# Expert base pass of 64 slots in two column tiles, with overflow passes as short conditional blocks

## The chip, the cores and the metric

One core of one Trainium2 chip. The metric is the device time of one execution in microseconds. Of the runs of a kernel the median is given.

## The reference, cut to what matters

One encoder block on 256 tokens of width 1024: sparse attention and a Mamba-2 mixer, then a mixture of experts. The change touches only the last part: top 4 of 32 experts per token, each a clamped SwiGLU of 1024 to 2 x 1024 to 1024, in fp32.

```
logits = (xt @ w_router + b_router).astype(jnp.float32)
top_val, top_idx = lax.top_k(logits, TOPK_EXPERTS)
gates = jax.nn.softmax(top_val, axis=-1)
...
h = xt[tok] @ w1[e] + b1[e]
gate, up = h[:, :D_FF_EXPERT], h[:, D_FF_EXPERT:]
gate = jnp.minimum(gate, SWIGLU_LIMIT)
up = jnp.clip(up, -SWIGLU_LIMIT, SWIGLU_LIMIT)
act = (up + 1.0) * gate * jax.nn.sigmoid(SWIGLU_ALPHA * gate)
y = act @ w2[e] + b2[e]
return acc.at[tok].add(y * g[:, None])
```

The 1024 assignments are not spread evenly. With the reference's inputs experts 0 to 31 get 23, 11, 12, 101, 28, 32, 37, 2, 41, 13, 36, 3, 18, 9, 10, 138, 47, 66, 16, 27, 21, 34, 28, 23, 51, 20, 31, 43, 37, 11, 40 and 15 tokens.

## The kernel before, in words

Attention and mixer come first; they and the router end where the stage of the experts begins. The weights of the experts, 12 MB each and 384 MB in all, are read from HBM once. They come as slabs of 1 MB through a ring of 17 buffers (`wa`, `wb`, `wc`): eight slabs of w1 (128 rows of 2048 columns) and four of w2. SP starts every load in the order of the program; `load_more(8)` stands where the w1 slabs of an expert are done with (L1659) and `load_more(4)` where its w2 slabs are (L1674). A load waits until PE has read the slab that had its buffer.

For one expert, `onehot` marks on DVE which token sits in which slot, `gather` (L1385) multiplies the tokens with that on PE into `xg`, two experts at a time, half of it in each expert, and `slots` (L1397) gives the matrix `sT` and the gates `gs` for the way back. The base pass takes T = 32 slots. `first_mm` (L1426) multiplies each w1 slab with the 32 columns of tokens as the stationary operand; its four matmuls lie in the four column tiles of PE and write one PSUM bank, `X[0]`. `swiglu` runs on DVE and ACT, `turn` (L1432) transposes, `second_mm` (L1438) multiplies with w2, again in four column tiles, into `X[1]` and `Y[1]`. `scale_y` (L1450) applies the gates on ACT and DVE, and `scatter` (L1456) adds the result to the four accumulators on PE. The scatter of one expert is done in the next one, behind its first product.

Tokens beyond slot 32 go through overflow passes: pass 1 takes slots 32 to 63 (32 columns), pass 2 slots 64 to 127 and pass 3 slots 128 to 191 (64 columns each); a rare block `rest` (L1515), behind expert 2, takes what lies beyond 192. The passes run under `tc.If` on the expert's count, which every engine loads into a register. `if_more` (L1507) nests them: pass 2 stands inside pass 1 and pass 3 inside pass 2, once for the first halves (name "a": gather, first product, swiglu, turn) and once for the second (name "b": second product, scatter). `will` (L1504) gives PE a hint ahead of a branch, which side it will take.

The program is written out in the order in which each engine runs it (`manual_schedule`). Where a block is not taken, an engine jumps over it, waits for its own last result, and adds to its semaphore what the block would have added; who depends on a block waits for that engine to have passed it.

Of the kernel before, what the change touches and what calls it, by code (L numbers as in the profile page):

```python
# [22 lines left out]
KD = 8  # L23
# [35 lines left out]
T = 32  # L59
# [5 lines left out]
def shape_constants():  # L65
# [6 lines left out]
    iota = np.tile(np.concatenate([p % 32 + 1, p % 64 + 1, p + 1]).astype(f32)[None, :], (P, 1))  # L72
# [20 lines left out]
def kernel(ctx, tc, A, out, dbg=None):  # L93
# [44 lines left out]
    cst = const.tile([P, 672], F32, name="cst")  # L138
# [5 lines left out]
    iota128 = cst[:, 512:640]  # L144
    fold = cst[:, 640:672]
# [255 lines left out]
    def small_b():  # L401
        small(cst2, A["cst"][:, 672:1184])
        small(cst3, A["cst"][:, 1184:1568])
        small(cst[:, 128:672], A["cst"][:, 128:672])
# [961 lines left out]
    def wide(nm, dt=F32):  # L1366
        return buf(nm, [512], dt, 4, "t2k")

    def act_tiles(spare):
        return (wide("go"), wide("so")) if spare else (buf("gu", [512]), buf("sgm", [256]))  # L1370

    aT = buf("aT", [256])
    aTs = {1: buf("aT1", [256]), 2: buf("aT2", [512]), 3: buf("aT3", [512])}
    xo = buf("xo", [KD, M])
    b1v = b1s.rearrange("p (g c) -> p g c", g=2)
    LOW = {1: T, 2: M, 3: 2 * M}
# [43 lines left out]
    def first_bias(e, h, m):  # L1420
        for c in range(4):
            t, j = h[c * m // P], c * m % P
            mm(t[j:j + m, :], lhsT=selc[:, e:e + 1].to_broadcast([96, m]), rhs=b1v[:, :, c * 256:c * 256 + 256],
               start=True, stop=False, skip_group_check=True)

    def first_mm(w, x, h, m, k):  # L1426
        for c in range(4):
            t, j = h[c * m // P], c * m % P
# [3 lines left out]
    def turn(us, h, a):  # L1432
        for i, u in enumerate(us):
            for c in range(2):
                tr(h[i][:, cut(c)], u[:, cut(c)], ident)
            act(a[:, i * 256:i * 256 + 256], h[i][:, 0:256], AF.Copy)  # L1436
# [13 lines left out]
    def scale_y(y, gs, tag=None):  # L1450
        v = [wide(nm, F32R) if tag else buf(nm, [512], F32R, 2) for nm in ("yh", "yl")]
# [9 lines left out]
    counts, hints = {}, {}  # L1461

    def load_count(e):
        counts[e] = nc.values_load(cnt[0:1, e:e + 1], min_val=0, max_val=256)
        for p in (1, 2, 3):
            hints[e, p] = counts[e] > LOW[p]
# [8 lines left out]
    def own_gather(e, base):  # L1475
        g = buf("hgo", [2, M])
        onehot(g, e, iota64[:, 0:M], base)
        gather(g, xo, 0, X[1], M)

    def more_first(e, p):  # L1480
        if p == 1:
            put = put_hot(e, iota32, T, "o")
            x, h, m = xs(e)[:, :, T:M], (Y[0],), T
        else:
            put = put_hot(e, iota64, LOW[p], "o")
            own_gather(e, LOW[p])
            x, h, m = xo, (Y[0], X[1]), M
        first_bias(e, h, m)
        for k in range(KD):
            first_mm(wt[e * 12 + k], x, h, m, k)  # L1490
        us = [swiglu(t, True) for t in h]
        more[e, p] = slots(e, put, Y[1], str(p), 1)
        turn(us, h, aTs[p])

    def more_second(e, p, nhs):
        m = T if p == 1 else M
        ys = X[1], Y[1]
        for nh in nhs:
            for k in range(KD):
                second_mm(w2_part(e, k, nh), ys[nh], aTs[p], m, k)  # L1500
        for nh in nhs:
            scatter(nh, more[e, p][0], scale_y(ys[nh], more[e, p][1], "t2k"))

    def will(e, nm, p=1):  # L1504
        tc.mark_branch_hint_location("%s%d_%d" % (nm, e, p), hint=hints[e, p], engines=[mybir.EngineType.PE])

    def if_more(e, nm, f, *a, p=1):  # L1507
        with tc.If(counts[e] > LOW[p], label="%s%d_%d" % (nm, e, p)):  # L1508
            if p < 3:
                will(e, nm, p + 1)  # L1510
            f(e, p, *a)
            if p < 3:
                if_more(e, nm, f, *a, p=p + 1)

    def rest(e, dw):  # L1515
        own_gather(e, FULL)
        sg = slots(e, put_hot(e, iota64, FULL, "o"), Y[1], "2", 1)
        h, a = (X[0], Y[0]), aTs[2]
        first_bias(e, h, M)
        for k in range(KD):  # L1520
            nc.sync.dma_start(dw, w1[e, cut(k), :])
            first_mm(dw.rearrange("p (g c) -> p g c", g=2), xo, h, M, k)
        turn([swiglu(t, True) for t in h], h, a)
        y = X[1], Y[1]
        for q in range(4):
            v = dw.rearrange("p (a n) -> p a n", n=D)
            nc.sync.dma_start(v, w2[e, q * 256:(q + 1) * 256, :].rearrange("(a p) n -> p a n", p=P))
            for k in range(2 * q, 2 * q + 2):
                for nh in range(2):
                    second_mm(v[:, k % 2, nh * 512:(nh + 1) * 512], y[nh], a, M, k)  # L1530
        for nh in range(2):
            scatter(nh, sg[0], scale_y(y[nh], sg[1], "t2k"))

    def gate_values():
        for tt in range(2):
# [3 lines left out]
            ex = buf("rex", [NE], bufs=2)  # L1539
# [6 lines left out]
        gr = buf("gr", [2, NE])  # L1546
# [8 lines left out]
    def res(tt, hf, eng):  # L1555
        cs = slice(hf * 512, (hf + 1) * 512)
        tmp = wide("ftmp")
# [6 lines left out]
    fin = {}  # L1564

    def fin_split():
        r, o = wt["fin"], ring2()
        fin[0], fin[1] = o[:, 0:D], o[:, D:2 * D]
        o = ring2()
# [181 lines left out]
```

## Time and profile before

| | us |
|---|---|
| median of 3 runs | 1521.59 |
| lowest, highest | 1519.45, 1529.33 |
| the profiled execution | 1524.34 |
| its span, first to last instruction | 1522.5 |

The profile is of one execution. PE is the matmul side of TensorE, PEld its weight loads, DVE VectorE, ACT ScalarE, POOL GpSimd, SP the engine that starts the loads; a q behind a name is the sequencer of the engine, which waits and branches. A matmul in fp32 shows as two records. L12 is line 12 of the kernel.

### The profile page before, as it was taken

What the parts mean: (1) busy time and instruction counts of PE and PEld (TensorE: products, weight loads), DVE (VectorE), ACT (ScalarE), POOL (GpSimd) and SP (SyncE); (2) the same over time, 40 slices, a digit from 0 to 9 for tenths busy, and PEclk for the clock granted to TensorE, in tenths of its full rate; (3) what the DMA queues carried; (4) which work ended last, traced back from release to release, by engine and by line L of the source; (5) the groups of instructions that cost most, each with busy time, mean ns of one, the idle gap of its engine ahead of it and who ended that gap; (6) DMA issues with size and microseconds to landing.
All of it is one profiled execution on the core that took longest, in us unless ns stands there. A gap on an engine that the chain in (4) does not pass through costs nothing. (4 is left out here: it accounts for less than half of the span.)

```text
span 1522.5 us, 21278 instructions
## 1 busy us (share of the span) xinstructions
PE 1225.6 (80%) x8399; PEld 666.2 (44%) x8399; DVE 537.1 (35%) x1107; ACT 294.1 (19%) x508; POOL 172.1 (11%) x123
## 2 busy tenths in 40 slices
PE   6988989998768878787777788988867777778784
PEld 3778778886323333334323243433332323323331
DVE  5678689786311212122212112221121212212134
ACT  2465546543100101010100001011000001001011
POOL 2333135423000000000000000000000000000002
PEclk9889989999978999899998869989998989989896
DMA  9777446987995699999999905465899999999971
GB/s 305 227 216 255 159 161 203 307 290 304 372 409 220 245 414 415 412 412 415 413 413 414 407 31 221 193 252 215 323 415 415 412 414 415 414 413 370 386 316 43
DMA packets 127430, 480.89 MB, mean 316 GB/s; under 512 B 12635, under 2 KB 49643, under 8 KB 92406
## 3 DMA queue, kind: packets, MB, share of 16 engines
q1 hardware_dynamic: 122598, 472.40, 79.3%
q10 hardware_dynamic: 4624, 5.67, 1.2%
q8 instruction: 137, 2.24, 0.6%
q14 instruction: 71, 0.58, 0.1%
HBM read 475.00 MB, written 3.03 MB: 314 GB/s over the span
## 5 line engine op out<-in xcount | busy, mean ns | idle before, releaser
L1429 PE MATMUL px<-wb,xg 128*32 128x512 f32 x1080 | 143.1, 646 | 28.4 <-DMA wb<-in_w 24.4
L1459 PE MATMUL acc<-yh,sT 128*128 128x512 f32 x192 | 95.4, 497 | 50.2 <-PEq L1508 39.5
L1395 POOL TENSOR_TENSOR xg<-xg,modT 128x512 f32<-128x512 f32 x32 | 33.3, 1040 | 875.9 <-DVE xg L1393 875.9
L1412 DVE TENSOR_SCALAR gu<-px 128x256 f32<-128x256 f32 x32 | 13.6, 425 | 303.5 <-PE px L1429 303.5
L426 PE MATMUL pj<-uTh,wl 128*128 128x256 f32 x360 | 106.9, 297 | 5.4 <-DVE wl L305 2.9
L426 PE MATMUL pj<-uTh,wh 128*128 128x256 f32 x360 | 108.6, 302 | 0.4 <-ACT iqz L645 0.4
L305 POOL TENSOR_TENSOR wl<-wa,wh 128x1024 fp32r<-128x1024 f32 x34 | 87.8, 2583 | 178.6 <-ACT wh L304 150.4
L426 PE MATMUL pj<-uTl,wh 128*128 128x256 f32 x360 | 106.4, 295 | 0.0
L1453 DVE SCALAR_TENSOR_TENSOR yl<-px,gs,yh 128x512 fp32r<-128x512 f32 x48 | 36.0, 751 | 198.1 <-ACT yh L1452 194.2
L304 ACT ACTIVATE wh<-wa 128x1024 fp32r<-128x1024 f32 x75 | 78.7, 1057 | 107.3 <-PE pj L426 77.7
L1459 PE MATMUL acc<-yl,sT 128*128 128x512 f32 x192 | 92.7, 483 | 4.5 <-DVEq L1508 3.1
L1414 ACT ACTIVATE sgm<-gu 128x256 f32<-128x256 f32 x32 | 13.3, 416 | 397.0 <-DVE gu L1412 397.0
L1459 PEld LDWEIGHTS acc<-yh,sT 128*128 128x128 f32 x192 | 43.6, 227 | 97.1 <-issue 54.1
L1429 PEld LDWEIGHTS px<-wb,xg 128*32 128x32 f32 x1080 | 34.6, 115 | 116.3 <-issue 68.4
L1443 PE MATMUL px<-wb,aT 128*32 128x512 f32 (+1 forms) x376 | 70.3, 600 | 17.0 <-ACT aT L1436 8.9
L1429 PE MATMUL px<-wa,xg 128*32 128x512 f32 x504 | 73.3, 685 | 11.4 <-DMA wa<-in_w 8.8
L1393 DVE TENSOR_TENSOR xg<-py,sc 128x512 f32<-128x512 f32 x32 | 22.1, 692 | 170.1 <-PE py L1389 99.0
L426 PEld LDWEIGHTS pj<-uTh,wl 128*128 128x128 f32 x360 | 72.6, 202 | 8.2 <-POOL wl L305 3.5
L1389 PEld LDWEIGHTS py<-hg,n 128*128 128x128 f32 x512 | 71.1, 213 | 11.2 <-issue 6.2
L426 PEld LDWEIGHTS pj<-uTh,wh 128*128 128x128 f32 x360 | 72.7, 202 | 4.0 <-issue 2.9
L1389 PE MATMUL py<-hg,n 128*128 128x128 f32 x512 | 69.8, 294 | 5.5 <-issue 2.5
L1429 PE MATMUL px<-wc,xg 128*32 128x512 f32 x464 | 62.8, 656 | 13.4 <-DMA wc<-in_w 13.4
(442 smaller groups left out, 2069.2 us busy)
## 6 DMA issues: line engine op xcount, KB each, us to landing
wb<-in_w SPq DMA_DIRECT2D x201, 1024.0 KB, 19.1
wc<-in_w SPq DMA_DIRECT2D x92, 1024.0 KB, 20.1
wa<-in_w SPq DMA_DIRECT2D x91, 1024.0 KB, 18.4
wa<-in_w_in SPq DMA_DIRECT2D x24, 1024.0 KB, 6.9
wa<-in_w_mod SPq DMA_DIRECT2D x16, 1024.0 KB, 5.0
wa<-in_w_mod SPq DMA_DIRECT2D x16, 512.0 KB, 6.1
wa<-in_w_proj_b SPq DMA_DIRECT2D x4, 1024.0 KB, 5.2
wa<-in_w_proj_a SPq DMA_DIRECT2D x4, 1024.0 KB
```

Of the source, the lines that this page charges most:

```text
L304: i = act(xh, x, AF.Copy)
L305: eng.tensor_tensor(xl, x, xh.bitcast(F32), op=OP.subtract)
L426: mm(o, lhsT=a[:, k, :], rhs=b[:, k, :], start=(k == 0 and i == 0), stop=(k == KD - 1 and i == 2), skip_group_check=True)
L1389: mm(t[:, i * m:(i + 1) * m], lhsT=n2[:, tt, cut(k0 + i)], rhs=oh[:, tt, :], start=(tt == 0), stop=(tt == 1), skip_group_check=True)
L1393: V.tensor_tensor(o, t.rearrange("p (a s) -> p a s", a=n), sc2[:, ks].unsqueeze(2).to_broadcast([P, n, m]), op=OP.mult)
L1395: G.tensor_tensor(o, o, sh2[:, ks].unsqueeze(2).to_broadcast([P, n, m]), op=OP.add)
L1412: V.tensor_scalar(gt, h[:, 0:w], SWIGLU_LIMIT, None, op0=OP.min)
L1414: act(sg, gt, AF.Sigmoid, scale=SWIGLU_ALPHA)
L1429: mm(t[j:j + m, :], lhsT=x[:, k, 0:m], rhs=w[:, :, c * 256:c * 256 + 256], start=False, stop=(k == KD - 1), skip_group_check=True)
L1443: mm(y[m * j:m * j + m, :], lhsT=a[:, b:b + m], rhs=w, start=(k < n), stop=(k >= KD - n), skip_group_check=True)
L1453: V.scalar_tensor_tensor(v[1], y, gs, v[0].bitcast(F32), op0=OP.mult, op1=OP.subtract)
L1459: mm(acc[tt][nh], lhsT=sT[:, tt, :], rhs=y, start=False, stop=False, skip_group_check=True)
```

## The change

The base pass takes M = 64 slots: four matmuls of 64 columns for each w1 slab, in two column tiles, into two PSUM banks `X[0]` and `Y[0]`, two swiglus, two turns. Pass 1 is gone. Passes 2 and 3 are no longer nested and carry no hints: each is three blocks in the first half (`more_in`: gather and slots; `more_first` for either bank) and one block in the second (`more_second`), with an `If` of its own around each. Pass 2's first half stands directly behind the base's first product, then come the scatter of the expert before, the gather for the next pair and the slots, then pass 3's first half, then `load_more(8)`, then the turns and the second product. In the last expert the scaling of the base's result comes ahead of the overflow blocks. Some buffers change: the pair gather goes through `X[1]` in place of `Y[0]`, `hg`, `sT` and `gs` are single, and a temporary of the last step lies in the ring. A constant of 128 columns that nobody read is gone.

```diff
-    LOW = {1: T, 2: M, 3: 2 * M}
+    LOW = {2: M, 3: 2 * M}
...
-    def first_mm(w, x, h, m, k):
-        for c in range(4):
-            t, j = h[c * m // P], c * m % P
-            mm(t[j:j + m, :], lhsT=x[:, k, 0:m], rhs=w[:, :, c * 256:c * 256 + 256], start=False,
+    def first_mm(w, x, h, k, phs=(0, 1)):
+        for c in range(2 * phs[0], 2 * phs[-1] + 2):
+            j = c % 2 * M
+            mm(h[c // 2][j:j + M, :], lhsT=x[:, k, 0:M], rhs=w[:, :, c * 256:c * 256 + 256], start=False,
                stop=(k == KD - 1), skip_group_check=True)
...
-    def second_mm(w, y, a, m, k):
-        n = P // m
-        j = k % n
-        c, q = k % 2, k // 2
-        b = q // n * 256 + c * P + q % n * m
-        mm(y[m * j:m * j + m, :], lhsT=a[:, b:b + m], rhs=w, start=(k < n), stop=(k >= KD - n), skip_group_check=True)
+    def second_mm(w, y, a, k):
+        j = k % 2
+        b = k // 4 * 256 + k % 2 * P + k % 4 // 2 * M
+        mm(y[M * j:M * j + M, :], lhsT=a[:, b:b + M], rhs=w, start=(k < 2), stop=(k >= KD - 2), skip_group_check=True)
...
-    def more_first(e, p):
-        if p == 1:
-            put = put_hot(e, iota32, T, "o")
-            x, h, m = xs(e)[:, :, T:M], (Y[0],), T
-        else:
-            put = put_hot(e, iota64, LOW[p], "o")
-            own_gather(e, LOW[p])
-            x, h, m = xo, (Y[0], X[1]), M
-        first_bias(e, h, m)
+        more[e, p] = slots(e, put, Y[1], str(p), 1)
+
+    def more_first(e, p, ph):
+        h = X[1], Y[1]
+        first_bias(e, h, (ph,))
         for k in range(KD):
-            first_mm(wt[e * 12 + k], x, h, m, k)
-        us = [swiglu(t, True) for t in h]
-        more[e, p] = slots(e, put, Y[1], str(p), 1)
-        turn(us, h, aTs[p])
+            first_mm(wt[e * 12 + k], xo, h, k, (ph,))
+        turn(swiglu(h[ph], True), h[ph], aTs[p], ph)
...
-    def if_more(e, nm, f, *a, p=1):
-        with tc.If(counts[e] > LOW[p], label="%s%d_%d" % (nm, e, p)):
-            if p < 3:
-                will(e, nm, p + 1)
+    def if_more(e, p, f, *a):
+        with tc.If(counts[e] > LOW[p]):
             f(e, p, *a)
-            if p < 3:
-                if_more(e, nm, f, *a, p=p + 1)
+
+    def more_a(e, p):
+        if_more(e, p, more_in)
+        for ph in range(2):
+            if_more(e, p, more_first, ph)
...
-        us = [swiglu(h)]
-        if_more(e, "a", more_first)
-        load_more(KD)
+        us = [swiglu(t) for t in h]
+        more_a(e, 2)
         if not last:
-            will(e, "b")
             for v in late:
                 scatter(*v)
             if q < NE // 2:
                 pair_gather(q, e % 2)
-        sT, gs = slots(e, put, Y[1], "", 2)
-        turn(us, (h,), aT)
+        sT, gs = slots(e, put, Y[1], "", 1)
+        more_a(e, 3)
+        load_more(KD)
+        for ph in range(2):
+            turn(us[ph], h[ph], aT, ph)
         if not last:
             for k in range(KD):
                 for nh in range(2):
-                    second_mm(w2_part(e, k, nh), y[nh], aT, T, k)
+                    second_mm(w2_part(e, k, nh), y[nh], aT, k)
             late = [(nh, sT, scale_y(y[nh], gs)) for nh in range(2)]
-            if_more(e, "b", more_second, (0, 1))
+            for p in (2, 3):
+                if_more(e, p, more_second, (0, 1))
             load_more(3 if e == LATE else 4)
```

What PE's program has at the end of the base's first product, before; `wc` and `wb` are w1 slabs, `xg` the gathered tokens, L1508 the branch of an `If`, L1738 the hint:

```order
L1423 MATMUL px_3648<-b1s,selc 32x512
L1429 MATMUL px_3648<-wc,xg 32x512 x12
L1429 MATMUL px_3648<-wb,xg 32x512 x20
L1508 COMPARE_AND_BRANCH
L1505 REGISTER_ALU
L1738 BRANCH_PREFETCH_HINT
L1423 LDWEIGHTS selc
L1423 MATMUL py_3650<-b1s,selc 32x512
```

and now, with the first of the eight branches (L1489) and the first rows of its block:

```order
L1425 MATMUL px_3648<-wb,xg 64x512 x2
L1425 MATMUL py_3650<-wb,xg 64x512 x2
L1489 COMPARE_AND_BRANCH
L1385 MATMUL px_3649<-hgo,n_78 128x64 x16
L1397 LDWEIGHTS hpo
L1397 MATMUL py_3651<-identb,hpo 128x128
```

The slabs feed 64 columns into two banks, by turns, and the block behind the branch begins with the gather of pass 2.

Where the first half of the overflow ends and the scatter begins on PE, before; `go` is the activation of a pass, `acc` an accumulator:

```order
L1435 MATMUL py_3650<-cst,go 128x128 x2
L1435 MATMUL px_3649<-cst,go 128x128 x2
L1508 UNCONDITIONAL_BRANCH x4
L1505 REGISTER_ALU
L1738 BRANCH_PREFETCH_HINT
L1459 MATMUL acc_3644<-yh,sT 128x512
```

and now, where the third of three blocks in a row ends:

```order
L1489 COMPARE_AND_BRANCH
L1419 LDWEIGHTS selc
L1419 MATMUL py_3651<-b1s,selc 64x512
L1419 LDWEIGHTS selc
L1419 MATMUL py_3651<-b1s,selc 64x512
L1425 MATMUL py_3651<-wc,xo 64x512 x4
L1425 MATMUL py_3651<-wb,xo 64x512 x12
L1430 MATMUL py_3651<-cst,go 128x128 x2
L1489 UNCONDITIONAL_BRANCH x2
L1452 MATMUL acc_3644<-yh,sT 128x512
```

One join at the end of a nest has become three joins one behind the other, and the same stands once more behind the slots.

SP's program for one expert, before; L1018 and L127 start the loads of w1 and w2 slabs:

```order
L1508 COMPARE_AND_BRANCH x3
L1508 UNCONDITIONAL_BRANCH x4
L1018 DMA wb<-in_w 128x2048 x4
L127 DMA wb<-in_w 128x2x1024 x2
L127 DMA wa<-in_w 128x2x1024 x2
L1508 COMPARE_AND_BRANCH x3
```

and now:

```order
L1489 COMPARE_AND_BRANCH
L1489 UNCONDITIONAL_BRANCH x2
L1016 DMA wa<-in_w 128x2048 x4
L126 DMA wc<-in_w 128x2x1024 x4
L1489 COMPARE_AND_BRANCH
L1489 UNCONDITIONAL_BRANCH x2
L1489 COMPARE_AND_BRANCH
L1489 UNCONDITIONAL_BRANCH x2
L1016 DMA wb<-in_w 128x2048 x4
```

The eight loads stand behind the last of six branches, which waits for what PE does behind scatter, gather and slots; before, they stood behind one nest that PE passed ahead of these.

## Rows read from the trace of the kernel before

**Rows 1.** The page, busy tenths of the DMA engines in 40 equal slices.
```profile
DMA  9777446987995699999999905465899999999971
```

**Rows 2.** Windows: stretch, length, busy PE, PEld, DVE, ACT, POOL; clock, DMA share, GB/s.
```profile
820.00:850.00 30.00, 21.94 (x130) 7.05 (x130) 4.59 (x11) 2.07 (x4) 1.04 (x1) 0.85 1.02 414
...
970.00:1000.00 30.00, 24.55 (x188) 11.13 (x180) 8.57 (x21) 4.25 (x8) 1.04 (x1) 0.94 0.65 261
1000.00:1030.00 30.00, 26.78 (x192) 12.46 (x194) 5.42 (x17) 1.22 (x3) 1.04 (x1) 0.83 0.43 177
1030.00:1060.00 30.00, 25.13 (x150) 11.52 (x150) 6.28 (x16) 3.83 (x8) 1.04 (x1) 0.94 0.50 193
```

**Rows 3.** Waits of SP's queue from 440 us on: total, times, longest.
```profile
SPq L1018 <- PEq L1508: 324.2, 34, 42.2
```

**Rows 4.** PE's timeline, experts 14 and 15: start, length, instruction [idle before <-releaser].
```profile
811.03 0.40 PE L1423 MATMUL px<-b1s,selc 96*32 96x512 bf16 x4 [0.83 <-PEq L1508]
...
841.05 0.40 PE L1423 MATMUL px<-b1s,selc 96*32 96x512 bf16 x4 [0.83 <-PEq L1508]
...
845.78 1.06 PE L1429 MATMUL px<-wb,xg 128*32 128x512 f32 x8 [1.42 <-DMA wb<-in_w]
```

**Rows 5.** PE's timeline, a 64-column overflow pass and a 32-column base pass.
```profile
914.40 1.02 PE L1429 MATMUL py<-wb,xo 128*64 128x512 f32 x4
915.26 1.02 PE L1429 MATMUL px<-wb,xo 128*64 128x512 f32 x4
...
965.78 3.61 PE L1429 MATMUL px<-wc,xg 128*32 128x512 f32 x32
```

**Rows 6.** PE's timeline, expert 14: end of the scatter, gather, start of the second product.
```profile
831.32 0.39 PE L1459 MATMUL acc<-yl,sT 128*128 128x512 f32 x1
831.55 1.95 PE L1389 MATMUL py<-hg,n 128*128 128x128 f32 x16
...
834.43 0.97 PE L1443 MATMUL px<-wa,aT 128*32 128x512 f32 x2 [0.52 <-ACT aT L1436]
```

**Rows 7.** Timeline: the first matmul behind a skip, in experts 3, 7 and 14.
```profile
498.65 0.49 PE L1459 MATMUL acc<-yh,sT 128*128 128x512 f32 x1 [0.63 <-PEq L1508]
...
626.15 0.79 PE L1459 MATMUL acc<-yh,sT 128*128 128x512 f32 x1 [2.95 <-PEq L1508]
...
829.61 0.49 PE L1459 MATMUL acc<-yh,sT 128*128 128x512 f32 x1 [0.41 <-PEq L1508]
```

**Rows 8.** Line 1508, branches of PE's sequencer: shortest/median/longest ns.
```profile
L1508 PEldq COMPARE_BRANCH  x119: 68/309/6337, 380.0 to 1501.5; - x119
```

**Rows 9.** The page's groups: busy us, mean ns | idle before.
```profile
L1412 DVE TENSOR_SCALAR gu<-px 128x256 f32<-128x256 f32 x32 | 13.6, 425 | 303.5 <-PE px L1429 303.5
```

**Rows 10.** PE's timeline, a scatter in expert 16.
```profile
981.76 0.63 PE L1459 MATMUL acc<-yl,sT 128*128 128x512 f32 x1
982.19 0.63 PE L1459 MATMUL acc<-yh,sT 128*128 128x512 f32 x1
```

**Rows 11.** PE's timeline, expert 15: pass 1, gathers of passes 2 and 3, their second halves.
```profile
860.68 0.65 PE L1423 MATMUL py<-b1s,selc 96*32 96x512 bf16 x4
...
872.76 5.14 PE L1389 MATMUL px<-hgo,n 128*128 128x64 f32 x32 [0.52 <-DVE hgo L1381]
...
900.32 7.09 PE L1389 MATMUL px<-hgo,n 128*128 128x64 f32 x32 [0.47 <-ACT aT L1436]
...
944.55 1.94 PE L1443 MATMUL px<-wb,aT 128*64 128x512 f32 x8
...
954.16 1.94 PE L1443 MATMUL px<-wb,aT 128*64 128x512 f32 x8
```

**Rows 12.** The first matmuls of the experts (first and last start), behind expert 2, and b2.
```profile
L1423 PE MATMUL px<-b1s,selc x136: 379/389/637, 375.4 to 1479.5; 96*32 96x512 bf16 x128, 96*64 96x512 bf16 x8
...
447.09 0.62 PE L1423 MATMUL px<-b1s,selc 96*32 96x512 bf16 x4 [9.32 <-DVEq L1680]
...
L1694 PE MATMUL acc<-wa,gTs 32*128 32x512 f32 x8 | 6.9, 1038 | 0.3 <-DVE gTs L1691 0.3
```

More of the change, by code (lines that the diff above doesn't have):

```diff
@@ L1448, in w2_part, with scale_y @@
         return wt[e * 12 + KD + nh * 2 + k // 4][:, k % 4, :]
-    def scale_y(y, gs, tag=None):
-        v = [wide(nm, F32R) if tag else buf(nm, [512], F32R, 2) for nm in ("yh", "yl")]
+    def scale_y(y, gs, v=None):
+        v = v or [buf(nm, [512], F32R, 2) for nm in ("yh", "yl")]
         act(v[0], y, AF.Copy, scale=gs)
@@ L1459, in scatter @@
                 mm(acc[tt][nh], lhsT=sT[:, tt, :], rhs=y, start=False, stop=False, skip_group_check=True)
-    counts, hints = {}, {}
+    counts = {}
     def load_count(e):
         counts[e] = nc.values_load(cnt[0:1, e:e + 1], min_val=0, max_val=256)
-        for p in (1, 2, 3):
-            hints[e, p] = counts[e] > LOW[p]
     more = {}
@@ L1499, in more_second @@
             for k in range(KD):
-                second_mm(w2_part(e, k, nh), ys[nh], aTs[p], m, k)
+                second_mm(w2_part(e, k, nh), ys[nh], aTs[p], k)
         for nh in nhs:
-            scatter(nh, more[e, p][0], scale_y(ys[nh], more[e, p][1], "t2k"))
-    def will(e, nm, p=1):
-        tc.mark_branch_hint_location("%s%d_%d" % (nm, e, p), hint=hints[e, p], engines=[mybir.EngineType.PE])
-    def if_more(e, nm, f, *a, p=1):
-        with tc.If(counts[e] > LOW[p], label="%s%d_%d" % (nm, e, p)):
-            if p < 3:
-                will(e, nm, p + 1)
+            scatter(nh, more[e, p][0], scale_y(ys[nh], more[e, p][1], yo))
+    def if_more(e, p, f, *a):
+        with tc.If(counts[e] > LOW[p]):
             f(e, p, *a)
-            if p < 3:
-                if_more(e, nm, f, *a, p=p + 1)
+    def more_a(e, p):
+        if_more(e, p, more_in)
+        for ph in range(2):
+            if_more(e, p, more_first, ph)
     def rest(e, dw):
-        own_gather(e, FULL)
+        g = buf("hgo", [2, M])
+        onehot(g, e, iota64[:, 0:M], FULL)
+        gather(g, xo, 0, X[1], M)
         sg = slots(e, put_hot(e, iota64, FULL, "o"), Y[1], "2", 1)
         h, a = (X[0], Y[0]), aTs[2]
-        first_bias(e, h, M)
+        first_bias(e, h)
         for k in range(KD):
             nc.sync.dma_start(dw, w1[e, cut(k), :])
-            first_mm(dw.rearrange("p (g c) -> p g c", g=2), xo, h, M, k)
-        turn([swiglu(t, True) for t in h], h, a)
+            first_mm(dw.rearrange("p (g c) -> p g c", g=2), xo, h, k)
+        for i in range(2):
+            turn(swiglu(h[i], True), h[i], a, i)
         y = X[1], Y[1]
@@ L1626, in pair_gather @@
     def pair_gather(q, half):
-        gather(hg[q].rearrange("p t e s -> p t (e s)"), xg[q], 4 * half, Y[0], 2 * M)
+        gather(hg[q].rearrange("p t e s -> p t (e s)"), xg[q], 4 * half, X[1], 2 * M)
     def xs(e):
@@ L1701 @@
         for k in range(KD):
-            second_mm(w2_part(e, k, nh), y[nh], aT, T, k)
-        will(e, "b%d_" % nh)
-        if_more(e, "b%d_" % nh, more_second, (nh,))
-        scatter(nh, sT, scale_y(y[nh], gs))
+            second_mm(w2_part(e, k, nh), y[nh], aT, k)
+        v = scale_y(y[nh], gs)
+        for p in (2, 3):
+            if_more(e, p, more_second, (nh,))
+        scatter(nh, sT, v)
         if nh == 0:
```

74 lines of the change are left out of this document (35 added, 39 removed).

## The prediction

> **What bounds the kernel now.** I read the page's slices first, then the windows, then PE's timeline expert by expert. In the slices [rows 1] the sixteen DMA engines stand at nine tenths or more over most of the expert stage, which begins near 375 us, with holes near 480, 880 to 1080 and at the end. The windows say the same in numbers [rows 2]: 820 to 850 moves 414 GB/s with TensorE busy 21.94 of 30 us, while 970 to 1060 moves 177 to 261 GB/s with TensorE busy 24.6 to 26.8. So two regimes take turns: weights arrive at full rate and PE waits for them, or PE works and SP, which starts the loads, waits for PE to pass an `If` (324.2 us in 34 waits [rows 3]).
>
> In the first regime one expert takes what its loads take. Two starts, those of experts 14 and 15, lie 30.0 us apart (811.03 and 841.05), and inside the expert PE waits for each megabyte, 1.42 us before the slab at 845.78 [rows 4]. Twelve slabs of 1.05 MB at 414 GB/s make 30.4 us; I take that as the pace of the loads. A base pass is hidden while PE needs less than this for an expert, and sets the time where it needs more. That is the whole question.
>
> Which experts overflow follows from the reference's inputs: 20 of the 32 have at most 32 tokens, 9 have 33 to 64, and experts 3, 15 and 17 have 101, 138 and 66.
>
> [...] An fp32 matmul stands in the trace as two records.
>
> Products. The base's first product has 32 matmuls, 64 records, in either kernel. Four 64-column records follow the last four after 0.86 us (914.40, 915.26), so 64 take 13.7 us with two column tiles at work; 32 records of 32 columns took about 3.4 us (the row's 3.61 less the overlap with the next), so 64 took 6.9 [rows 5]. The second product has 32 records, so 6.9 us against 3.4. The base grows by 10.3 us for each of 32 experts, 330 us; the 12 passes over slots 32 to 63 go, each with the same 10.3 us and some waits. On PE's account that is a loss, since 20 experts never had that pass.
>
> The rest of an expert, from an undisturbed one [rows 6]: scatter 8 x 0.23 = 1.9; gather, slots, transposes and the wait for aT together 2.9 (831.55 to 834.43, less rounding), with 0.2 for two transposes more; bias 0.4, twice the 0.2 of four 32-column ones.
>
> Skips. An expert of up to 32 tokens passed two skips on PE, now eight, in groups of three, three and two. On the path not taken each engine first waits for its own last result, so PE is empty in a group. One skip that went well left PE idle 0.41 us (829.61), one followed by a second branch instruction 0.63 (498.65) [rows 7]; ahead of the next expert it was 0.83 [rows 4]. PE's branches take 309 ns in the median [rows 8]; with 0.2 for the semaphore step between two of them I count 0.5 for each further skip, so 1.4, 1.4 and 1.3: 4.1 us. Bounds: 1.6 if only the first of each group shows (0.41 + 0.41 + 0.83), and 2.5 more for every group that meets a slow branch, from 626.15, where the same skip left 2.95 instead of 0.41. I take 4.1, nearer to the quick rows, since the median is quick.
> [...]
>
> Sum for one expert: 0.4 + 13.7 + 1.4 + 1.9 + 2.9 + 0.2 + 1.4 + 6.9 + 1.3 = 30.1 us, already the pace of the loads, and two things are missing. First, the gather writes a buffer that the conditional blocks also read, so it waits until DVE has passed the first group; DVE stands there behind two swiglus now, not one. A swiglu is four DVE steps of some 0.42 us [rows 9], 1.7 us; two end about when PE has done its skips and the scatter. I take 0.5 us (bounds 0 and 1.7). Second, the clock. After short idle times the granted clock falls: at 981.76 and 982.19 the scatter steps by 0.43 us and not 0.23 [rows 10], and in 970 to 1060, where PE sets the pace, the mean granted clock is 0.94, 0.83 and 0.94 [rows 2]. I count one scatter per expert at 1.2 GHz, 1.5 us; bounds 0, and 5 if scatter, gather and transposes all run at half. So an interval of 32.1, taken as 32, and the loads lie beside it.
>
> The release of the eight w1 slabs moves behind scatter, gather, slots and six branches, some 6 us later in SP's program, with SP's next eight loads queued behind it. With PE as the bound this costs nothing: five slabs of the next expert are in the ring by then, and the three missing ones have the second product's 6.9 us and the first five slabs' 8.6 us to land. If PE is not the bound, the first expert alone holds its slabs some 10 us longer while the ring is full.
>
> Overflow from slot 64 on: four passes run, as now. One costs 27.6 us in its first half (two gathers at 872.76 and 900.32) and 9.6 in its second (944.55 to 954.16) [rows 11]; the split by column half exposes one more swiglu step chain, about 1 us net, and the skip time of some 2 us goes: 36 us each, 144.
>
> The path through PE: first expert at 375.4 [rows 12]; 31 intervals of 32 are 992, to 1367; overflow 144, to 1511; the jump over `rest` behind expert 2, which left PE idle 9.32 us, adds 8 beyond an ordinary group, to 1519; the eight b2 matmuls 6.9, to 1526. The last expert took 43.0 us (1479.5 to the span's end, 1522.5); it gains 10.3 of base work, loses some 3 of branch waits: 50, to 1576. Expert 0 has no scatter and the last two no gather, 5.6 us together: 1570. The profiled execution took 1524.34 us for its span of 1522.5, so 1572, and lies 2.75 above the median of the runs, 1521.59, so 1569.
>
> **Rivals.**
> A, the loads still set the pace. If the later skips of a group hide and the clock stays up, PE needs 28 us, under the loads' 30.4. Then the first expert (10 us) and the last (about 8) show, less some 8 of slow branches that go where PE sets the pace now: about 1530. For it: the sum without skips is 26 us. Against it: every row with a second branch has its gap, and the base, 20.6 us of products where 10.3 stood, leaves no room for a slow clock. [...]
>
> B, slow branches without the hints. Now 119 branches have a median of 309 ns but a maximum of 6337 [rows 8]. If one group in each expert meets that, PE loses 2.5 us more per expert: 32 x 2.5 = 80, so 1649. For it: slow ones exist even with hints. Against it: the jumps are short now, over one block of product, and not over three.
> [...] No run shows a short jump alone yet.
>
> C, faster. In the stretches that PE sets (experts 3, 15 to 17 and 21: five of the 12 removed passes) each pass that goes frees 10.3 us of products and some 7 of exposed steps (12.1 us from 860.68 to 872.76 less 6.9 of matmuls [rows 11], and a scatter of 1.9): 85 us. If the larger bases of the same experts and of the two or three behind them find their slabs landed and no skip gap, they give back some 60 of it: 25 us net, 1497. It decides only where PE's time for an expert stays under about 28 us. Against it: the experts that catch up behind expert 17 then need 10 us more each.
>
> **How the numbers follow.** Forecast 0.62, A 0.14, B 0.18, C 0.04, anything else 0.02. A measurement here tells about 1% from no change, 1506 to 1537. C is faster, 0.04; A and what lies under an interval of 31 us are the same, 0.15; the rest, 0.81, is slower. The forecast's own range is 1538 to 1615, intervals of 31 to 33.5. The range goes down through A to 1518 and up to B's 1650.
>
> **What would show it.** Right: ordinary experts start about 32 us apart from the first on; PE has hardly any wait for a slab in the base's first product; the DMA share is near 0.95, with a short hole in each expert; about 1.4 us idle on PE at each group of three; 64 records in 13.7 us. A is right if PE still waits for slabs all through. B is right if PE's branch row has many of several us. The forecast is wrong if starts lie 30.4 us apart, or if a group of branches leaves less than 0.7 us.

## The result, and the profile after

The changed kernel takes 1583.76 us in the median of four runs (1580.01 to 1584.52), the kernel before 1521.55 beside it: a ratio of 1.039, interval 1.035 to 1.043. It is slower by 62 us; 1569 was forecast, with a range that holds it. The profiled execution took 1584.52 for a span of 1582.7.

The page after, PE's busy time and the tenths of PE, granted clock and DMA in 40 slices:

```profile
PE 1337.2 (84%) x7095; PEld 769.5 (49%) x7095; DVE 541.4 (34%) x1115; ACT 291.0 (18%) x524; POOL 173.1 (11%) x123
...
PE   6788989998878898888888888888888888888884
...
PEclk9989989999997999999999989989999999999898
DMA  9667547974895479999999933472799999999970
```

PE is busy at eight tenths from the first expert to the last; the DMA row has its holes around the same experts as before [rows 1]. The windows of before [rows 2], and one of an ordinary stretch, in the same columns:

```profile
820.00:850.00 30.00, 26.31 (x128) 13.22 (x130) 4.60 (x12) 2.36 (x5) 1.04 (x1) 0.94 1.01 411
970.00:1000.00 30.00, 24.27 (x111) 8.81 (x111) 5.43 (x12) 4.79 (x10) 0.00 (x0) 1.00 0.72 280
1000.00:1030.00 30.00, 27.87 (x127) 10.96 (x127) 6.00 (x17) 2.21 (x4) 0.00 (x0) 1.00 0.34 140
1030.00:1060.00 30.00, 24.50 (x124) 11.92 (x124) 6.83 (x19) 2.76 (x6) 1.04 (x1) 0.98 0.90 363
1208.00:1238.00 30.00, 26.30 (x132) 12.98 (x131) 5.99 (x15) 2.62 (x7) 1.04 (x1) 1.00 1.02 415
```

At 820 PE has 26.31 us of work in 30 and not 21.94, and the clock stands at 0.94 to 1.00 where it had been 0.83 to 0.94. What is left of the 30 us is this, in PE's timeline of expert 21 (start, length, instruction, idle before and its releaser):

```profile
1208.11 0.43 PE L1419 MATMUL px<-b1s,selc 96*64 96x512 bf16 x2 [0.94 <-PEq L1489]
...
1208.54 1.08 PE L1425 MATMUL px<-wb,xg 128*64 128x512 f32 x4
1209.40 1.08 PE L1425 MATMUL py<-wb,xg 128*64 128x512 f32 x4
...
1223.61 0.47 PE L1452 MATMUL acc<-yh,sT 128*128 128x512 f32 x1 [1.11 <-PEq L1489]
1223.92 0.40 PE L1452 MATMUL acc<-yl,sT 128*128 128x512 f32 x1
1224.15 0.39 PE L1452 MATMUL acc<-yh,sT 128*128 128x512 f32 x1
...
1225.59 2.02 PE L1385 MATMUL px<-hg,n 128*128 128x128 f32 x16
...
1229.29 0.41 PE L1430 MATMUL px<-cst,gu 128*128 128x128 f32 x2 [1.53 <-PEq L1489]
...
1230.17 1.08 PE L1436 MATMUL px<-wa,aT 128*64 128x512 f32 x4 [0.26 <-ACT aT L1431]
...
1238.49 0.43 PE L1419 MATMUL px<-b1s,selc 96*64 96x512 bf16 x2 [1.18 <-PEq L1489]
```

Nothing waits for a slab. Three gaps are left, 1.11, 1.53 and 1.18 us, one at each group of skips; the scatter steps by 0.23 us, at a granted clock of 1.00 (1223.60 to 1225.60). PE's waits from 380 us on (total, times, longest), the branches (shortest/median/longest ns) and SP's wait that answers to [rows 3]:

```profile
PE px L1430 <- PEq L1489: 50.4, 31, 4.5
PE acc L1452 <- PEq L1489: 29.5, 27, 1.3
PE px L1419 <- PEq L1489: 27.7, 28, 1.2
```
```profile
L1489 PEldq COMPARE_BRANCH  x274: 70/208/3737, 388.7 to 1566.0; - x137
```
```profile
SPq L1016 <- PEq L1489: 536.1, 52, 47.2
```

The 60.2 us between the two profiled spans, by the first matmul of each expert (an interval runs from one expert's start to the next):

| | before | after | |
|---|---|---|---|
| start of expert 0 | 375.4 | 378.7 | +3.3 |
| 26 intervals without a long expert | 762.4 | 813.4 | +51.0 |
| expert 2, with the jump over `rest` | 33.1 | 37.6 | +4.4 |
| expert 3 (101 tokens) | 80.6 | 75.1 | -5.5 |
| expert 15 (138) | 122.8 | 109.5 | -13.3 |
| expert 17 (66) | 73.6 | 74.5 | +0.9 |
| expert 29, with the b2 matmuls | 31.5 | 39.7 | +8.2 |
| last expert, to the end | 43.0 | 54.2 | +11.2 |

The long experts gain 18 us; the 26 ordinary ones lose 51. Their mean goes from 29.32 to 31.28 us. Before, this mean was made of quick experts of 17 to 27 us and of slower ones, up to 49 us with pass 1; now the fastest of the 26 takes 29.65 us.

### The profile page after: what moved, and what is told of

It is laid out like the page before. It is cut to its first block, busy times and chain, and to the rows that moved or that the text cites. A ratio compares the mean times of both kernels' runs of the same rounds, so it can differ in the third digit from the quotient of the medians.

```text
span 1582.7 us, 19858 instructions
## 1 busy us (share of the span) xinstructions
PE 1337.2 (84%) x7095; PEld 769.5 (49%) x7095; DVE 541.4 (34%) x1115; ACT 291.0 (18%) x524; POOL 173.1 (11%) x123
## 5 line engine op out<-in xcount | busy, mean ns | idle before, releaser
L1425 PE MATMUL px<-wb,xg 128*64 128x512 f32 x540 | 148.3, 599 | 0.0
L1425 PE MATMUL py<-wb,xg 128*64 128x512 f32 x540 | 147.9, 598 | 0.0
L1408 DVE TENSOR_SCALAR gu<-px 128x256 f32<-128x256 f32 x32 | 13.6, 425 | 363.9 <-PE px L1425 363.9
L1436 PE MATMUL px<-wb,aT 128*64 128x512 f32 x288 | 84.1, 641 | 9.3 <-issue 3.9
L1425 PEld LDWEIGHTS py<-wb,xg 128*64 128x64 f32 x540 | 53.4, 138 | 64.2 <-issue 62.6
L1436 PE MATMUL py<-wb,aT 128*64 128x512 f32 x296 | 83.5, 620 | 0.0
L1425 PEld LDWEIGHTS px<-wb,xg 128*64 128x64 f32 x540 | 53.3, 139 | 57.3 <-issue 54.6
L1452 PE MATMUL acc<-yh,sT 128*128 128x512 f32 x128 | 54.9, 429 | 31.1 <-PEq L1489 29.5
L424 PEld LDWEIGHTS pj<-uTl,wh 128*128 128x128 f32 x360 | 71.7, 199 | 1.2 <-issue 0.8
L1385 PE MATMUL px<-hg,n 128*128 128x128 f32 x512 | 67.2, 286 | 5.1 <-DVEq L1489 3.9
L1385 PEld LDWEIGHTS px<-hg,n 128*128 128x128 f32 x512 | 62.9, 199 | 15.8 <-ACTq L1489 10.8
L1425 PE MATMUL px<-wa,xg 128*64 128x512 f32 x252 | 69.0, 604 | 0.0
```

The source lines that it names most:

```text
L424: mm(o, lhsT=a[:, k, :], rhs=b[:, k, :], start=(k == 0 and i == 0), stop=(k == KD - 1 and i == 2), skip_group_check=True)
L1385: mm(t[:, i * m:(i + 1) * m], lhsT=n2[:, tt, cut(k0 + i)], rhs=oh[:, tt, :], start=(tt == 0), stop=(tt == 1), skip_group_check=True)
L1408: V.tensor_scalar(gt, h[:, 0:w], SWIGLU_LIMIT, None, op0=OP.min)
L1425: mm(h[c // 2][j:j + M, :], lhsT=x[:, k, 0:M], rhs=w[:, :, c * 256:c * 256 + 256], start=False, stop=(k == KD - 1), skip_group_check=True)
L1436: mm(y[M * j:M * j + M, :], lhsT=a[:, b:b + M], rhs=w, start=(k < 2), stop=(k >= KD - 2), skip_group_check=True)
L1452: mm(acc[tt][nh], lhsT=sT[:, tt, :], rhs=y, start=False, stop=False, skip_group_check=True)
```

## The experiments

The kernel before was run again beside each experiment; its medians lie between 1520.7 and 1526.8 us, so a difference of a few microseconds between two experiments is not clear by itself.

**Fewer skips.** One `If` around each pass's first half.

```diff
-        if_more(e, p, more_in)
-        for ph in range(2):
-            if_more(e, p, more_first, ph)
+        if_more(e, p, more_all)
```

> The changed kernel with the three blocks of each overflow pass's first half under one If, so that an ordinary expert passes four skips in groups of one, one and two, where the changed kernel has eight in groups of three, three and two. Theory S (PE sets the pace, and each further skip costs PE about 0.5 us): PE's time for an ordinary expert falls by some 2 us, from 31.3 to 29.3, under the loads' 30.4, and the starts lie 30.4 to 30.6 us apart; 26 such intervals and the last expert give about 22 us, so 1555 to 1568. Rival R (the late release of the w1 slabs behind scatter, gather and slots sets the pace, and skips are only waited through): no change beyond 5 us, since the release stands where it stood. Rival B (slow branches without hints): the ten branches of over 1 us become about half as many, 10 us faster, and the ordinary interval without one stays above 30.

1538.88 us, 45 less, twice what was expected. Intervals have a median of 28.8 us, below the pace of the loads. The gap ahead of the scatter is gone altogether:

```profile
1180.23 0.47 PE L1452 MATMUL acc<-yh,sT 128*128 128x512 f32 x1
...
1182.88 2.02 PE L1385 MATMUL px<-hg,n 128*128 128x128 f32 x16 [0.56 <-DVEq L1489]
```

PE's sequencer had taken the single branch 9.9 us into the expert, at 1175.59, while matmuls were still queued until 1180.08; the join followed at 1180.12. In the changed kernel's expert 21 the first of three branches comes as early, at 1218.00, but the other two start only behind the matmuls' end, at 1222.69 and 1223.10. Part of what the missing gap gave is lost again in the row shown: the gather now waits 0.56 us for DVE to have passed its branch (27 such waits, 17.8 us together). Slow branches also became fewer, 6 of 14.5 us together against 9 of 19.0. That the interval falls under the pace of the loads (30.2 us, measured in the next pair) contradicts my floor; the next pair shows why.

**No overflow at all, wide and narrow base.** The blocks and their `If`s are taken out of the changed kernel, and out of the kernel before.

```diff
-        if_more(e, p, more_in)
-        for ph in range(2):
-            if_more(e, p, more_first, ph)
+        return
...
-            for p in (2, 3):
-                if_more(e, p, more_second, (0, 1))
```

> The changed kernel without any overflow block or its If: tokens beyond the first 64 of an expert are left out. Theory S: PE's time for an expert is then 27 to 28 us, less than the loads' 30.4, so after the first experts every interval is 30.4 us and PE waits for slabs again; 379 + 31 x 30.4 + 50 = 1371, with up to 8 for the jump behind expert 2: 1371 to 1385. Rival R: the release of the w1 slabs behind scatter, gather and slots still leaves holes in the transfers, and intervals stay above 31 us: 1395 or more. Rival W (the wide base alone is too long for PE, with or without skips): intervals of 31 us or more with PE busy through and no wait for slabs, also 1395 or more; the waits of PE tell it from R.

> The kernel before (base of 32 slots) without any overflow block or its If: tokens beyond the first 32 of an expert are left out. It gives the pace of the loads with nothing in their way, to set beside the changed kernel without its overflow. Theory S: intervals of 30.4 us all through, first start 375, last expert 40: 375 + 31 x 30.4 + 40 = 1357, 1350 to 1370; the wide base without overflow lies about 10 to 15 us above, all of it in the first and the last expert. Rival W (the wide base is too long for PE by itself): the distance is 35 us or more. A third reading, that the 30.4 us of the kernel before were partly its branch waits: intervals of under 30 us, below 1345.

1350.52 and 1340.47 us: the wide base alone costs 10 us. Both sums were too long, by 17 us and by 20 at the least, and the windows of the wide one show why (stretch, length, PE, PEld, DVE, ACT, POOL, clock, DMA share, GB/s):

```profile
500.00:560.00 60.00, 59.48 (x300) 34.90 (x298) 12.67 (x34) 5.52 (x12) 2.08 (x2) 1.00 1.02 416
...
800.00:860.00 60.00, 53.97 (x264) 24.89 (x263) 12.37 (x34) 5.18 (x13) 2.08 (x2) 1.00 1.02 416
```

The transfers run at 416 GB/s in both. At 500 PE is busy throughout, the starts of experts 4 to 9 lie 26.3 us apart; at 800 it waits for slabs and they lie 30.2 apart. So a wide expert without skips needs 26.3 us of PE, and while the ring of 17 slabs is ahead, PE goes at its own speed and not at the loads'. In the narrow one expert 0 takes 13.6 and expert 1 15.8 us. A stall of the loads fills the ring, and a base that is faster than 30.2 us earns the stall back over the following experts. The third reading falls: the narrow kernel's later intervals lie mostly at 30.2 to 30.6.

**The release of the w1 slabs earlier.** Twice: in the changed kernel, and in the one with four skips.

```diff
         more_a(e, 2)
+        more_a(e, 3)
+        load_more(KD)
...
-        more_a(e, 3)
-        load_more(KD)
```

> The changed kernel with pass 3's first half and the release of the eight w1 slabs moved ahead of scatter, gather and slots, directly behind pass 2's first half: the same blocks and the same eight skips, six of them in one group. It undoes the move of the release alone. Theory S (PE sets the pace): no gain, 1575 to 1592; the six skips in a row may leave 1 us more or less idle than two groups of three. Rival R (the late release sets the pace): the loads start some 6 us earlier in each expert, intervals fall to 30.4, 20 us or more faster: 1564 or less, and the holes in the transfers shrink.

> The changed kernel with one If around each pass's first half, as in the run with four skips, and with pass 3's first half and the release of the eight w1 slabs ahead of scatter, gather and slots: groups of two and two. The move of the release alone, without six skips in a row. Theory S: PE's time for an expert is what it was, 28.7 us, and in stretches in which the loads lead it changes nothing; where slabs are short, PE gains up to 6 us once. Within 10 us of the run with four skips, 1530 to 1549. Rival R (the late release is a cost of its own): 1520 or less. If the idle of the double skip drops the clock of scatter and gather as behind the six skips (0.43 us for a scatter's step and not 0.23): 1550 or more.

1639.71 and 1536.58. With four skips the move is worth 2 us of 1538.88, nothing; the late release is no cost, rival R falls. In the changed kernel the same move costs 56, and neither theory had that. What is new in it is that six skips stand in a row. PE's timeline of two experts of it:

```profile
1196.86 0.77 PE L1452 MATMUL acc<-yh,sT 128*128 128x512 f32 x1 [6.66 <-PEq L1489]
1197.42 0.63 PE L1452 MATMUL acc<-yl,sT 128*128 128x512 f32 x1
1197.85 0.63 PE L1452 MATMUL acc<-yh,sT 128*128 128x512 f32 x1
...
1229.83 0.47 PE L1452 MATMUL acc<-yh,sT 128*128 128x512 f32 x1 [2.56 <-PEq L1489]
```

Six skips that go well leave 2.56 us idle, three left 1.11: 0.48 for each further one. But in 12 of 27 ordinary experts one of the branches takes 2 to 4.7 us (4.4 in the first row's group), and behind such idle times the scatter steps by 0.43 us and not 0.23: 131 of its 224 steps against 13 of 241 in the changed kernel, where the granted clock in 0.43-us steps is 0.50 (1089.9 to 1091.6). Slow branches take 39.8 us here and 19.0 there, so they are 21 of the 56 us; 118 further steps of the scatter at 0.43 and not 0.23 us make about 24 more, an estimate.

**How far, or how many?** The six in a row again, with shorter blocks.

```diff
-        for k in range(KD):
+        for k in (0, KD - 1):
             first_mm(wt[e * 12 + k], xo, h, k, (ph,))
```

> The changed kernel with its release moved ahead of scatter, gather and slots (six skips in a row), with shorter overflow blocks: the first product of passes 2 and 3 takes only the first and the last of the eight w1 slabs, so tokens beyond slot 64 get a wrong product. The six skips then pass over 72 matmuls of PE's program and not 120. In the runs so far a skip group ahead of the scatter had a branch of over 1 us in 0 of 27 experts over 60 matmuls in three skips, 12 of 27 over 120 in six, 17 of 27 over 120 in two, 9 of 28 over 120 in one, 24 of 27 over 162 in seven. Theory F (a slow branch comes from how far PE jumps, by one branch or several): 0 to 5 slow groups of 27, the group takes 2.5 us from its first branch on in the mean and not 3.65, ordinary intervals near 32; with some 40 us off the four overflow passes, 1530 to 1575. Rival N (it comes from the number of branches in a row): 10 or more slow groups of 27, 1580 to 1600.

1536.82 us in one run, and no branch was slow. This kernel leaves out six of the eight w1 slabs in the overflow passes, and experts 3, 15 and 17 are 40 us shorter for it; the other 63 us less than the six in a row with whole blocks lie in the rest.

```profile
L1489 PEldq COMPARE_BRANCH  x274: 70/208/443, 389.1 to 1518.5; - x137
```

The same 274 branches, none over 0.45 us. By 27 ordinary experts of the kernels with a wide base, the skip group ahead of the scatter alone:

| matmuls passed over | skips | experts with a branch over 1 us |
|---|---|---|
| 60 | 3 (changed kernel) | 0 |
| 60 | 1 (one `If`) | 0 |
| 72 | 6 | 0 |
| 120 | 1 (nest, below) | 10 |
| 120 | 2 | 17 |
| 120 | 6 | 12 |

In these runs branches became slow with the amount of the program that is passed over; rival N, the number of branches in a row, falls. The distance within one group is not the whole rule: the 9 slow branches of the changed kernel all stand in its second group, which passes over 60 matmuls again some 2.4 us after the first, and with one `If` there only 2 experts had one ahead of the same transposes. What was passed over shortly before seems to count too; no run separates that.

What a slow branch goes with is in the traces. The page of the changed kernel counts packets of 16 KB of the kind "instruction" (packets, MB, share of 16 engines):

```profile
q8 instruction: 130, 2.13, 0.5%
```

In the kernel before, the changed one and the ten experiments with an `If`, all 166 branches of these `If`s that took over 1 us ended 1.3 to 1.6 us behind the landing of one such packet; of the 1993 quicker ones 64 did. So I read a slow branch as a wait for program code; the traces show the two together, not why. PE's idle time without a releaser can follow such a packet too; the longest in the changed kernel, in expert 5, ends 1.4 us behind one:

```profile
609.35 1.98 PE L1436 MATMUL px<-wb,aT 128*64 128x512 f32 x4 [3.16 <-issue]
```

By the table short jumps in a row add up: over 120 matmuls 12 of 27 groups were slow with six jumps, 10 with one. Which part of the program a branch waited for is not on record.

**The short blocks with the narrow base.**

The base of 32 slots is kept, and pass 1 becomes one block, passes 2 and 3 three blocks each. All seven stand in one group ahead of the scatter, without hints; in the change the two passes' blocks stand apart.

```diff
+        if_more(e, 1, more_one)
+        for p in (2, 3):
+            if_more(e, p, more_in)
+            for ph in range(2):
+                if_more(e, p, more_half, ph)
```

> The kernel before with its base of 32 slots, but the overflow passes as flat blocks without hints (pass 1 one block in the first half, passes 2 and 3 three each, one behind the other behind the base's first product; three blocks behind the second): ten skips in an ordinary expert, in groups of seven and three. The structure of the change alone, without its wide base. From the changed kernel with its release moved (2.56 us for a group of six that went well, 0.42 us for each further skip, 6.7 where a branch was slow) the groups cost about 3.0 and 1.4 us. Theory S in its second form (the time is set by the loads plus what the long experts stop them for; a base is free as long as PE's time for an expert is under the loads' 30.2 us, and under that it catches up): PE needs about 20 + 4.4 = 24 to 25 us, still well under 30.2, so the skips cost next to nothing in ordinary experts and some 4 us in each of the five or six long ones: 1520 to 1550. Rival (skips stop the loads by themselves, through SP's own branches or through slow branches of PE): like the changed kernel, 1560 or more.

1615.14 us, 94 over the kernel before, far outside what I expected. Seven skips pass over 162 matmuls here, and 24 of 27 groups had a slow branch; PE's longest waits for them:

```profile
PE acc L1459 <- PEq L1519: 178.1, 27, 10.9
```

6.6 us for a group, where 3.0 was assumed: the price of a good group was taken and the chance of a bad one left out. So flat blocks put in a row on the narrow base cost more than the whole change. How much the change's own order would cost with 32 slots was not run.

**Hints, and the nest with a wide base.** The kernel before without its hints; and the changed kernel with the passes nested and hinted as before and the release behind the nest.

```diff
-        tc.mark_branch_hint_location("%s%d_%d" % (nm, e, p), hint=hints[e, p], engines=[mybir.EngineType.PE])
+        pass
```

> The kernel before without PE's branch hints, all else the same. In the kernel before 24 of PE's 119 branches took over 1 us, 118 us together, with the hints there; in the changed kernel, without hints but with short blocks, 10 of 274, 25 us. Theory S (a slow branch comes from the length of the jump, and where the loads set the pace it is covered): within 1% of the kernel before, 1510 to 1540, with about as many slow branches. Rival B (the hints hold slow branches off): 30 or more branches of over 1 us, and what falls into experts 3, 15 to 17 and 21 and their neighbours shows: 20 to 40 us slower.

```diff
+            if p < 3:
+                will(e, nm, p + 1)
             f(e, p, *a)
+            if p < 3:
+                if_more(e, nm, f, *a, p=p + 1)
```

> A base of 64 slots as in the changed kernel, but its two overflow passes nested and hinted as in the kernel before, with the release of the w1 slabs directly behind the nest: an ordinary expert passes one skip ahead of the scatter and one behind the second product. The wide base alone, without the short blocks. Theory S in its second form: PE needs 26.3 us (the changed kernel without any overflow, where PE caught up) and 0.4 and 0.8 for the skips, 27.5; some 1.2 less than with four skips (1538.9), so it catches up faster behind each long expert: 1515 to 1535. Rival W (the wide base is what costs; it is never hidden): 1545 or more. Rival L (long jumps bring slow branches: 24 in the kernel before): more branches over 1 us than the 7 with four skips, and 1535 to 1560.

1541.21 (ratio 1.014, interval 1.009 to 1.019) and 1537.26. Without hints the kernel before has 37 branches of over 1 us, 201 us together, against 23 and 111, so the hints there hold off 14 slow branches and are worth 20 us: rival B's slow branches are real where jumps are long. The wide base in a nest needs 28.4 us for an ordinary expert, where 27.5 was expected, and is no faster than the one with four short skips: 14 of its 77 branches were slow, 40 us together. That is rival L.

**Both column halves, the one-hot matrix early, and a nest of the second halves.** On the kernel with four skips: first the two halves of an overflow pass together as before; then pass 2's one-hot matrix made ahead of the base's swiglus; then also the second halves nested.

```diff
-        turn(swiglu(h[ph], True), h[ph], aTs[p], ph)
+        us = [swiglu(t, True) for t in h]
+        more[e, p] = slots(e, put, Y[1], str(p), 1)
+        for ph in range(2):
+            turn(us[ph], h[ph], aTs[p], ph)
...
         put = put_hot(e, iota64, 0, "")
+        early[e] = own_hot(e, 2)
...
+    def if_second(e, nhs):
+        with tc.If(counts[e] > LOW[2]):
+            more_second(e, 2, nhs)
+            if_more(e, 3, more_second, nhs)
```

> The run with four skips (one If around each pass's first half), with the first product of an overflow pass over both column halves before its two swiglus, and the pass's slots behind them, as in the kernel before. It undoes the split by column half. In the run with four skips PE waited 1.85 us for a swiglu twice in each pass. Theory S: each of the four passes gets 2 to 2.5 us shorter, 8 to 10 us: 1525 to 1533. Rival O (the loads' lead takes it up, since what an overflow expert costs the loads is not its PE time alone): no change, 1534 to 1542.

> The version put together, with the second halves side by side again (four skips in an ordinary expert and not three): the early one-hot matrix alone, on top of the kernel with both column halves. The version with both edits took 1503.1 and its profile gave 66.3, 99.6 and 62.6 us for experts 3, 15 and 17 where the one with neither had 73.1, 104.5 and 69.1: 18 us from there, and 9 us from the ordinary intervals. Theory K (the wait of 2.8 us and the low clock behind it cost some 6 us in each of three passes): experts 3, 15 and 17 stay short, and 18 us of the 27 are there: 1509 to 1516. Rival (the missing skip gives most, as the ordinary intervals and the last expert follow PE): 1517 to 1526.

> A version put together from the runs so far: one If around each pass's first half (60 matmuls passed over at a time, with scatter and gather between the two), both column halves ahead of the swiglus, and in addition the second halves nested, so that an ordinary expert passes three skips and not four, and the one-hot matrix for pass 2's gather made ahead of the base's swiglus on DVE in every expert, where PE waited 2.8 us for it in each of three passes. Theory S: 0.42 us less in each of 26 ordinary intervals, 11 us, as far as they follow PE and not the loads, and some 8 us in experts 3, 15 and 17, off 1530.6: 1512 to 1522, which is 0 to 1% under the kernel before. Rival O (the loads' pace of 30.2 us over the whole stage bounds what the base can give back): 1525 to 1532, no difference from the kernel before.

1530.55, 1510.64 and 1503.10 us. The first gives 8 us as expected, and experts 3, 15 and 17 are 7.9 us shorter in it. The second gives 20 and not the 8 that I had first put on it, and these rows say why; expert 17 without it:

```profile
1026.93 5.93 PE L1385 MATMUL px<-hgo,n 128*128 128x64 f32 x32 [2.81 <-DVE hgo L1377]
...
1034.83 1.97 PE L1425 MATMUL py<-wb,xo 128*64 128x512 f32 x4 [0.48 <-POOL xo L1391]
1036.59 1.92 PE L1425 MATMUL px<-wb,xo 128*64 128x512 f32 x4
```

and with it (and the nest):

```profile
1007.95 3.79 PE L1385 MATMUL px<-hgo,n 128*128 128x64 f32 x32
...
1013.71 1.08 PE L1425 MATMUL py<-wb,xo 128*64 128x512 f32 x4 [0.71 <-POOL xo L1391]
1014.61 1.03 PE L1425 MATMUL px<-wb,xo 128*64 128x512 f32 x4
```

The wait of 2.81 us was followed by a gather of 5.93 us and a first product that steps by 1.76 us for four records; without the wait the gather takes 3.79 us and the step is 0.90. In the changed kernel the granted clock behind the same wait is 0.50 (1058.97 to 1066). With the early matrix alone experts 3, 15 and 17 go from 73.2, 104.5 and 69.1 to 63.9, 101.5 and 62.2 us. The nest of the second halves takes the ordinary interval's median from 29.2 to 28.6 us, and 7.5 us off the time. With one `If` and all three the kernel is faster than the changed one and the one before: 1503.10 against 1524.05 for the kernel before beside it, a ratio of 0.986, interval 0.983 to 0.989.

## Why the prediction was right, and where it was off

- **The question was the right one.** PE's time for an ordinary expert went over the loads' 30.2 us (30.4 in the prediction), and 51 of the 60 us are there. Starts lie 31.28 us apart, PE waits for no slab, and each group of skips shows its gap, as named in what would show the forecast right. One sign named against it comes close, though: 16 of the 26 ordinary intervals have no slow branch and no long unreleased idle time, and their mean is 30.5 us, next to the 30.4 that would have spoken for the loads. That PE waits for no slab decides it.
- **Products, scatter, bias:** 64 records in 13.7 us and the scatter at 0.23 stand as worked out; without skips an expert needs 26.3 us, where the terms of the sum other than skips give 26.0.
- **Skips:** 1.4 + 1.4 + 1.3 forecast, 1.11 + 1.53 + 1.18 measured in expert 21, and 1.1, 1.6 and 1.0 in the mean of the waits above. One further skip measured 0.48 us, 0.5 forecast: the branch takes 208 ns in the median here, and from its end to the start of the next one pass 0.21 us, the median of 64 such pairs.
- **Clock and DVE:** the two terms that made 32 of 30 were wrong. The clock fell in no scatter of an ordinary expert (the 13 of 241 steps of 0.43 us are in experts 3, 15 and 17), and the gather followed the scatter without idle time; the wait for DVE came only with one `If`, 0.56 us. The mean of 31.28 has slow branches in their place: 9 in ordinary experts, 19 us together. 26 x (32 - 31.28) = 19 us too much in the sum. No run shows the 1.2 GHz of the clock term; what the traces show is a granted clock of 0.50 with steps of 0.43 us (before, 982 to 984) and of 1.00 with steps of 0.23.
- **Overflow:** 4 x 36 = 144 forecast. Over an interval of 31.28 experts 3, 15 and 17 take 43.8, 78.2 and 43.3: 165, so 41 for a pass. The step that failed is that four passes run "as now", with "about 1 us net" for the split. The 27.6 and 9.6 us were read from passes that stood behind pass 1; pass 2 now stands behind the base and takes waits that pass 1 had taken. Expert 17, pass 2's gather and the start of the second halves, before and after:

```profile
1017.49 6.38 PE L1389 MATMUL px<-hgo,n 128*128 128x64 f32 x32 [0.52 <-DVE hgo L1381]
...
1056.98 1.48 PE L1443 MATMUL px<-wc,aT 128*32 128x512 f32 x10 [1.62 <-DVE yl L1453]
...
1063.15 2.79 PE L1443 MATMUL px<-wc,aT 128*64 128x512 f32 x12
```
```profile
1058.97 7.09 PE L1385 MATMUL px<-hgo,n 128*128 128x64 f32 x32 [2.81 <-DVE hgo L1377]
...
1105.27 2.80 PE L1436 MATMUL px<-wc,aT 128*64 128x512 f32 x12 [1.52 <-DVE yl L1446]
```

  The wait for the one-hot matrix is 2.81 and not 0.52 us; 1.52 stand ahead of the second product, where pass 1 had the 1.62; and the split makes the two waits for a swiglu 1.85 and 1.91 where they were 0.81 and 1.22. That is 5.5 us in this pass, and with the same waits in experts 3 and 15 (2.88 and 1.52, 2.81 and 1.53) 16 us in the three, of which the forecast had 3. Undoing the split gave 8 us over all four passes. The 20 us of the early matrix are not all missing from the sum: the row of 27.6 us already held a gather of 5.14 us, at a granted clock of 0.71, where it takes 3.79 with the early matrix and the nest.
- **First and last expert:** the last took 54.2 us where 50 was forecast; the start was 3.3 later. The 5.6 us taken off for experts without a scatter or a gather did not come: experts 0 and 30 took 31.2 and 31.1.
- These errors have both signs: too much in the ordinary experts, too little in the passes and at the end, which left the forecast 15 us low. That the number came so near is in part luck; the mechanism, PE over the loads' pace through products and skips, is what the runs bear out.
- **Rival A** was priced by a floor that isn't one: "the loads still set the pace". With 28.8 us for an expert PE catches up behind every stall, and the price of the skips was 45 us and not the 22 that a floor of 30.4 leaves.
- **Rival B** took the hint for the cause. Unhinted short jumps were quick (no slow branch ahead of the scatter in 27 experts over 60 or 72 matmuls); what it foresaw came where I moved six of them together.
- **Rival C** had its gains where it said, in the long experts (18 us of the 85), and its losses larger.

## What to carry to other kernels

Ask of a change to a stage with a ring of loads not only whether compute exceeds the loads' pace, but how far below it stays: that margin paid back the stalls here (26.3 us without skips against the loads' 30.2). Count conditional blocks by what their skips expose: in expert 21 the first of a group was decided at 1218.00 while matmuls were still queued, the further ones at 1222.69 and 1223.10 behind a join, 0.48 us for each; and keep short what is jumped over in a row (0 of 27 groups slow over 72 matmuls, 10 to 17 over 120). Scatter, gather and slots between two groups were not enough in the changed kernel, where 9 of 27 second groups had a slow branch. Ask also which waits the first conditional block takes for those behind it: without it the next one takes them (2.81 us for the one-hot matrix in expert 17, 0.52 behind pass 1). A wait ahead of matmuls costs more than itself where the clock falls behind it (the 2.81 us, and a gather of 5.93 and not 3.79), so prepare small operands before the engine that makes them is busy with something else.

## What the runs showed that I had not expected

- A single skip leaves no idle time ahead of the next matmul where its branch is taken while matmuls are queued (0 ahead of the scatter with one `If`), a further one 0.48 us.
- Slow branches went with the distance of all jumps in a group: 0 of 27 over 72 matmuls, 10 to 17 of 27 over 120, 24 of 27 over 162. Every slow branch in all runs ended 1.3 to 1.6 us behind the landing of a packet of the kind "instruction".
- Behind idle times of 2.4 us the clock fell in some experts and not in others, in the run with short blocks (steps of the scatter of 0.43 us behind 2.41, of 0.23 behind 2.44); which it will be, no run here settles. Neither do they settle how what is passed over in one group acts on the next. Nor was it tried whether hints would help the short blocks.
